# Order of the matmul engine's instructions in a hybrid decoder step: scheduled against written out

## The chip, the cores and the metric

The kernel runs on one core of a Trainium2 chip. The metric is the device time of one execution in microseconds (us). The engines are TensorE (PE, with its weight loads listed apart as PEld), VectorE (DVE), ScalarE (ACT), GpSimd (POOL) and SyncE (SP, which only issues DMAs here). Each engine works through its own instructions in the order in which the built program has them, and waits at an instruction until the semaphores that it needs have their value.

## The reference

One step of a decoder layer, for a prompt of 512 tokens and, separately, 8 decode sequences of 4 tokens. Both share the weights, so the kernel runs the projections on 544 columns. All data is float32.

```python
u = jnp.einsum('btd,dc->btc', x, w_in)            # 2048 x 18952: 13 parts side by side
h_m, C, n, m = _mlstm(q_m, k_m, v_m, ig, lf, C0, n0, m0)   # 4 heads of 512, matrix memory C
h_a = _swa_prompt(q_a, k_a, v_a, slopes, sinks)   # 32 heads of 64, window 128, 4 KV heads
hn = layernorm_per_head(h_m) * mlstm_norm_w
y = (sigmoid(g_m) * ((hn * sigmoid(o_m) * silu(z_m)) @ w_proj_m)
     + sigmoid(g_a) * ((h_a * silu(z_a)) @ w_proj_a))
out = layernorm(2 ** 0.25 * x + y @ w_out) * ln_w + ln_b
```

The decode sequences use the same formulas with a state C of 512 x 512 per sequence and head (32 of them, 1 MB each), which is read, updated and written, and with a window of 128 stored keys and values.

## The kernel before

**Precision.** Every operand of a large product is split into a high part in a reduced format and a low part, the remainder: ACT casts (`wh`, L188) and DVE subtracts (`wl`, L189). A product is then hi x hi, hi x lo and lo x hi, that is three matmuls.

**The long stage.** After a prologue, in which values and keys of the attention (L514 to L529) and the gates are projected, `paired()` (L627) works through 72 pairs of weight column blocks. A pair multiplies two blocks of 128 columns at once with seven products in place of eight (a Strassen scheme). So it has seven steps, numbered 0 to 6, with the moving operands `a11`, `s1`, `n2`, `xk` (first half), `n3`, `s4`, `xk` (second half). `half_product()` (L582) issues one step: 16 matmuls with `wh` (L593, "hi") and 8 with `wl` (L595, "lo"), each of 272 columns. Steps 0, 1, 3 and 5 accumulate in the two banks of a PSUM tile X (step 0 and 3 in the first, 1 and 5 in the second); steps 2, 4 and 6 in a tile Y. `gather()` (L597) takes the results out: L604 after step 0 (`p`), L612 after 1, L615 after 2, L617, L619, L621 and L623 (the last, after 6). `prepare()` (L563) makes `wh` and `wl` of a step up to three steps ahead; there are two buffers of each.

The pairs carry a list of work: 16 query pairs (their end, `end_qz` L754, makes the query tiles `q` by L763 and L764 and the gate `sz` by L768 and L769), merge gates, and values, keys, queries and output gates of the four mLSTM heads.

**Work between the steps.** `tick()` (L126) runs after each step and lets every live generator go one `yield` further. Three generators matter. `attentions()` (L774) takes the 16 query pairs in turn: `attention()` (L682) handles two heads, a = 0 and 1. For each head it computes scores of four query blocks j, two of them in one PSUM tile of the pool `psB` (four buffers): two matmuls per block (L700), and DVE's read with bias, minimum and sink (L702). Exponentials (L711) and division (L717) on ACT, transposes (L728) and the product with the values (L738) follow some ticks later. `samples()` (L1093) runs `sample_head()` (L1040) for the decode states: per state four matmuls with the state (L1073), four outer products (L1079) and their additions to the state (L1080), with a DMA of the next state and stores of the last. `gates_` computes the gates once.

**What sets the order.** A scheduler with a timing model orders the instructions of every engine by priority and by when it expects operands. `high_priority(offset=...)` raises the priority of a block, `issue_after(...)` adds an edge that puts instructions behind a given one on the same engine. In `tick()` such an edge keeps the small work behind the last matmul of the step just issued (`state["end"]`); later than that it may slip freely, and the steps themselves may be interleaved. DMAs are issued from SP in order.

**After the long stage** come the attention's output projection with the prompt's mLSTM in its ticks, the merge, the last projection and the layernorm. The change does not touch their code.

Of the kernel before, what the change touches and what calls it, by code (L numbers as in the profile page):

```python
# [22 lines left out]
NB = 8  # L23
# [50 lines left out]
def _build(tc, nc, i, o, es):  # L74
# [11 lines left out]
    V, A, G, PE = nc.vector, nc.scalar, nc.gpsimd, nc.tensor  # L86
# [12 lines left out]
    def nm(s):  # L99
        count[0] += 1  # L100
        return f"{s}_{count[0]}"

    def sm():
        return psB.tile([128, 512], F32, tag="sm", name=nm("sm"))
# [10 lines left out]
    def blk(ap, n=4):  # L115
        return ap.rearrange("p (b x) -> p b x", b=n)


    live = []

    def spawn(g):
        live.append(g)

    state = {}

    def tick():  # L126

        with ExitStack() as place:
            if state.get("end"):
                place.enter_context(tc.issue_after(state["end"].ins))  # L130
            for g in list(live):
                if next(g, StopIteration) is StopIteration:
                    live.remove(g)

    def drain():
        while live:
            tick()
# [137 lines left out]
    for g in range(4):  # L275
# [9 lines left out]
        for q in range(4):  # L285
# [4 lines left out]
            k = g * 4 + q  # L290
# [156 lines left out]

    def attn_values(kk, vt):

        pt, pt2 = sm(), sm()  # L450
        for b in range(4):
            PE.transpose(pt[:, b * 128:b * 128 + 128], vt[:, b * 128:b * 128 + 128], ident)
        PE.transpose(pt2[:32, 0:128], vt[:, SEQ:T], ident)
        cs = slice(kk * 128, kk * 128 + 128)
        vr, vs = ev(512), ev(128)
        A.copy(vr[:], pt[:])
        V.tensor_copy(vs[:32], pt2[:32, 0:128])
        nc.sync.dma_start(d_vr[0:SEQ, cs].rearrange("(b p) c -> p b c", p=128), blk(vr[:]))
        nc.sync.dma_start(d_vr[SEQ:T, cs], vs[:32])
        nc.sync.dma_start(vb_p[0].rearrange("t k d -> t (k d)")[:, cs], vr[:, 384:512])  # L460

    def attn_keys(kk, kt):
        nc.sync.dma_start(d_ka[kk], kt[:])
        pt = sm()
        PE.transpose(pt[:, 0:128], kt[:, 384:512], ident)
        PE.transpose(pt[:32, 128:256], kt[:, SEQ:T], ident)
        cs = slice(kk * 128, kk * 128 + 128)
        kr = ev(256)
        V.tensor_copy(kr[:, 0:128], pt[:, 0:128])
        V.tensor_copy(kr[:32, 128:256], pt[:32, 128:256])  # L470
        nc.sync.dma_start(kb_p[0].rearrange("t k d -> t (k d)")[:, cs], kr[:, 0:128])
        nc.sync.dma_start(d_ks[:, cs], kr[:32, 128:256])
# [41 lines left out]
    for kk in range(2):  # L514
        ps = gemm(win, VA_ + kk * 128, xh, xl, raws=((raw0[0], raw0[1]), (raw0[2], None))[kk], every=4, prio=150 * kk,
                  before=gates_between if kk else None)
        if kk == 0:
            spawn(x_sums())
            gates_ps = mm()
        vt = ev()  # L520
        with ahead_of_sums():
            A.copy(two(vt[:]), pv(ps))
            attn_values(kk, vt)
    for kk in range(2):
        ps = gemm(win, KA + kk * 128, xh, xl, every=4, prio=150)
        kt = ev()
        with ahead_of_sums():
            A.copy(two(kt[:]), pv(ps))
            attn_keys(kk, kt)  # L529
    drain()  # L530
    for src, dst in ((d_ks, kb_s), (d_vr[SEQ:T], vb_s)):
        nc.sync.dma_start(dst[:, 124:128].rearrange("b t k d -> b t (k d)"), src.rearrange("(b t) c -> b t c", t=NTS))
# [49 lines left out]
    def half_product(w, n):  # L582
        bank = BANK[n]
        if n == 0:
            w["X"] = mm()
        if n == 2:
            w["Y"] = mm()
        ps = w["Y"][:, 0, :HT] if bank == 2 else w["X"][:, bank, :HT]
        wh, wl = w.pop(("hl", n))
        x, first = XS[n], n in (0, 1, 2)  # L590
        for k in range(8):
            for p in range(2):
                PE.matmul(ps, wh[:, k], x(p, k), start=(first and k == 0 and p == 0), stop=False, skip_group_check=True)  # L593
        for k in range(8):
            state["end"] = PE.matmul(ps, wl[:, k], x(0, k), start=False, stop=(k == 7), skip_group_check=True)  # L595

    def gather(w, n):  # L597

# [175 lines left out]
    def attentions():  # L774
        while gates_ in live:
            yield
        for _ in last:
            pass
        esG.close()
        sp["pz"] = pool(esQ, "pz", 1)  # L780
        open_attention()
        state["open"] = True
        for k in range(16):
            if k % 4 == 0:
                kv = kv_head(k // 4)
            while k not in waiting:
                yield
            yield
            yield
            yield from attention(k, *waiting.pop(k), kv)  # L790
            state["done"] = k + 1
        esB.close()
        yield from sample_attention()
        esT.close()
        open_samples()
        state["samples"] = True
# [224 lines left out]
    def sample_finish(h, r, pC):  # L1021
        qc = w512()
        A.activation(qc[:], pC[:], AF.Copy, scale=colT2[:, 4, 1, h:h + 1])
        gs = st1([128, 4, NS], "gs", p="sw")
        nc.sync.dma_start(gs[:], d_g[h * 4:h * 4 + 4, :, SEQ:T].rearrange("c p t -> p c t"))
        yield
        num, den = r["num"], r["den"]
        pI = sm()
        PE.matmul(pI[:NS, :], cc[:, C_SEL:C_SEL + 32], qc[:], start=True, stop=True)
        V.tensor_tensor(out=num, in0=pI[:NS, :], in1=num, op=ALU.add)  # L1030
        hn = w512()[:32]
        layernorm_rows(NS, den[:, 9:10], colT2[0:32, 4, 0, h:h + 1], [num], hn, sp["sw"])
        yield
        pt = sm()
        for c in range(4):
            PE.transpose(pt[:, c * 32:c * 32 + 32], hn[:, c * 128:c * 128 + 128], ident[:32, :32])
        V.tensor_tensor(out=gs[:], in0=blk(pt[:, 0:128]), in1=gs[:], op=ALU.mult)
        nc.sync.dma_start(d_brm[h * 4:h * 4 + 4, :, SEQ:T].rearrange("c p t -> p c t"), gs[:])

    def sample_head(h):  # L1040
        r = {}
        nxt = load_C(h, 0)
        yield from sample_prep(h, r)
        pC, stores = None, []

        def store():

            with tc.issue_after(state["load"].ins):
                for dst, src in stores:
                    nc.sync.dma_start(dst, src)  # L1050
            stores.clear()

        for b in range(NB):
            ct = nxt

            qz = st1([128, 4, NS], "qz", p="sw")
            G.memset(qz[:], 0.0)
            G.tensor_copy(qz[:, :, b * 4:b * 4 + 4], r["qs"][:, :, b * 4:b * 4 + 4])
            Ab = st1([128, 512], "Ab", F32R)
            G.tensor_scalar(Ab[:], r32(r["kA"][:]), cc[:, C_M8 + b:C_M8 + b + 1], None, op0=ALU.mult)  # L1060
            for j in range(4 + b % 2):
                yield
                if j == 0:
                    store()
                elif j == 2 and b + 1 < NB:
                    with tc.issue_after(state["load"].ins):
                        nxt = load_C(h, b + 1)
            if b == 0:
                pC = sm()

            with tc.high_priority(offset=3000):
                for c in range(4):
                    PE.matmul(pC[c * 32:c * 32 + 32, :], qz[:, c], ct[:, c],  # L1073
                              start=(b == 0), stop=(b == NB - 1), tile_position=(0, c * 32))
            for c in range(4):
                if c == 2:
                    yield
                pu = sm()
                PE.matmul(pu[:], Ab[:, c * 128:c * 128 + 128], r["V4"][:], start=True, stop=True)  # L1079
                V.scalar_tensor_tensor(ct[:, c], ct[:, c], dcb[:, h, b:b + 1], pu[:], op0=ALU.mult, op1=ALU.add)  # L1080
                if c % 2:
                    stores.append((C_s[b, h, (c - 1) * 128:c * 128 + 128, :].rearrange("(c p) v -> p c v", p=128),
                                   ct[:, c - 1:c + 1]))
        yield
        store()
        while h not in gated:
            yield
        yield from sample_finish(h, r, pC)
# [75 lines left out]
    work = [fill.pop(0) for _ in range(3)]  # L1164
# [11 lines left out]
    last = last_sum(s4)  # L1176
# [1 line left out]
    spawn(gates_)  # L1178
    spawn(attentions())
    spawn(samples())  # L1180
    paired(work, last)
    state["end"] = None
    drain()

    def branch(src, p, tmp, ahead=()):

# [186 lines left out]
    for ct in range(16):  # L1373
        sg = c5t()
        nc.sync.dma_start(sg[:], d_sga[ct])
        ps = gemm(wa_, ct * 128, bah, bal, every=2)
# [12 lines left out]
    for ct in range(16):  # L1389
# [3 lines left out]
        ps = gemm(wm, ct * 128, bmh, bml)  # L1393
# [136 lines left out]
    for ct in range(16 - G3):  # L1530
# [5 lines left out]
        ps = gemm(wo, ct * 128, yh, yl, cols=CUT, raws=raws)  # L1536
# [6 lines left out]
    for g in range(G3):  # L1543
        ct = 16 - G3 + g
        ps = sm()
        for half in range(2):
            raw = load_half(wo, ct * 128, half)
            if g < 2:
                wh, wl = (w[:, :, g] for w in w2[half])
                hilo(raw[:], wh, wl)  # L1550
            else:
                w1.append(split(raw))
                wh, wl = w1[half]
# [39 lines left out]
```

## Time and profile before

| quantity | us |
|---|---|
| median of three runs | 2601.6 |
| lowest and highest run | 2598.32, 2604.69 |
| profiled execution, own time | 2600.3 |
| its span, first to last instruction | 2598.5 |

The profile is of one execution. Its page lists busy time per engine. Views of the trace give the same for chosen stretches (windows), the waits between engines (who waited for which line's result: us in total, times, longest), and the instructions in order of time (timeline). A matmul's end in the trace is modelled: matmuls of one stream overlap in the listing, and the distance of their starts is what a matmul costs. Busy time of PE therefore holds some 0.15 us beyond the point at which a next matmul could have started.

In the long stage a step of 24 matmuls follows the next, with small groups of matmuls of the generators between or, where the scheduler chose so, inside them.

### The profile page before, as it was taken

To read this page: it belongs to the slowest core of one execution; us is meant where nothing else is said; L and a number is where in the kernel's file an instruction comes from. 1 tells how busy PE (TensorE), PEld (TensorE's weight loads), DVE (VectorE), ACT (ScalarE), POOL (GpSimd) and SP (SyncE) were. 2 spreads that over 40 slices of the span, in tenths; PEclk is the share of its full clock that TensorE was granted. 3 is DMA by queue.
4 is the path that set the end of the run, shared out by engine and by line. 5 is a ranking of instruction groups with operands and counts; after the bars stand their busy time and mean duration, and the time that the engine had idled before them with its cause. 6 is when DMAs were issued, how large, how long until landed. Compare 5 with 4: busy or idle time off the path is not lost.

```text
span 2598.5 us, 48858 instructions
## 1 busy us (share of the span) xinstructions
PE 2539.5 (98%) x19994; PEld 2469.6 (95%) x19994; DVE 1711.2 (66%) x2508; ACT 1176.7 (45%) x1908; POOL 359.9 (14%) x334
## 2 busy tenths in 40 slices
PE   8999999999999999999999999999999999999997
PEld 8999999999999999999999998999999999999997
DVE  7867667676676777587777777777766553333335
ACT  4447666666666665343433443434633332222221
POOL 2111111111111111121112222211000000000002
PEclk9999999999999999999999999999999999999999
DMA  6566656666665655457577566576755455445432
GB/s 194 136 150 160 151 138 155 150 145 144 151 151 138 149 133 146 107 179 229 163 219 235 151 207 212 157 229 200 222 181 172 156 170 163 132 140 178 116 93 90
DMA packets 537103, 421.86 MB, mean 162 GB/s; under 512 B 43536, under 2 KB 449344, under 8 KB 536592
## 3 DMA queue, kind: packets, MB, share of 16 engines
q1 hardware_dynamic: 526800, 382.04, 49.8%
q0 software_dynamic: 10080, 36.70, 8.2%
q8 instruction: 157, 2.57, 0.4%
q14 instruction: 66, 0.54, 0.1%
HBM read 297.66 MB, written 86.42 MB: 148 GB/s over the span
## 4 chain that ended last, share of the span: by engine, by line
PE 61%; DVE 2%; ACT 1%; issue 0%; DVEq 0%; ACTq 0%
PE mm L197 21%; PE mm L593 20%; PE mm L595 9%; PE sm L1256 2%; PE sm L1079 1%; PE sm L1073 1%; PE sm L1288 1%; PE sm L1301 1%; ACT wh L188 1%; PE sm L197 1%; DVE raw L570 0%; DVE z L1495 0%; PE sm L898 0%; PE sm L897 0%; PE sm L1235 0%
## 5 line engine op out<-in xcount | busy, mean ns | idle before, releaser
L188 ACT CAST wh<-raw 128x1024 fp32r<-128x1024 f32 x604 | 632.7, 1049 | 989.2 <-PE mm L593 568.2
L189 DVE TENSOR_TENSOR wl<-raw,wh 128x1024 fp32r<-128x1024 f32 x604 | 765.2, 1272 | 443.0 <-ACT wh L188 425.3
L593 PE MATMUL mm<-xk,wh 128*128 128x272 f32 x2304 | 314.4, 288 | 3.4 <-ACT ev L612 2.4
L593 PEld LDWEIGHTS mm<-xk,wh 128*128 128x128 f32 x2304 | 298.5, 188 | 8.0 <-ACT ev L612 3.1
L570 DVE TENSOR_TENSOR raw<-raw,raw 128x1024 f32<-128x1024 f32 x218 | 267.0, 1228 | 4.8 <-DMA raw<-in_w_in 2.6
L197 PE MATMUL mm<-bh,wl 128*128 128x272 f32 x1024 | 214.1, 289 | 0.0
L197 PE MATMUL mm<-bh,wh 128*128 128x272 f32 x1024 | 213.6, 290 | 0.0
L197 PE MATMUL mm<-bl,wh 128*128 128x272 f32 x1024 | 213.3, 288 | 0.0
L613 POOL TENSOR_TENSOR ev<-p,ev 128x272 f32<-128x272 f32 x72 | 103.6, 1439 | 588.4 <-ACT ev L612 562.5
L593 PE MATMUL mm<-n2h,wh 128*128 128x272 f32 x576 | 154.6, 300 | 25.0 <-ACT wh L188 24.7
L595 PE MATMUL mm<-xk,wl 128*128 128x272 f32 x1152 | 173.9, 288 | 0.0
L197 PEld LDWEIGHTS mm<-bh,wh 128*128 128x128 f32 x1024 | 160.7, 188 | 2.3 <-issue 2.3
L197 PEld LDWEIGHTS mm<-bl,wh 128*128 128x128 f32 x1024 | 161.3, 188 | 0.0
L197 PEld LDWEIGHTS mm<-bh,wl 128*128 128x128 f32 x1024 | 160.9, 189 | 0.0
L595 PEld LDWEIGHTS mm<-xk,wl 128*128 128x128 f32 x1152 | 155.7, 188 | 0.4
L593 PE MATMUL mm<-s1h,wh 128*128 128x272 f32 x576 | 151.0, 294 | 4.0 <-ACT p L604 4.0
L593 PE MATMUL mm<-n3h,wh 128*128 128x272 f32 x576 | 150.3, 290 | 0.2 <-DVE ev L615 0.2
L593 PE MATMUL mm<-n3l,wh 128*128 128x272 f32 x576 | 150.3, 291 | 0.0
L593 PE MATMUL mm<-n2l,wh 128*128 128x272 f32 x576 | 150.1, 292 | 0.0
L593 PE MATMUL mm<-s4h,wh 128*128 128x272 f32 x576 | 149.0, 290 | 1.1 <-ACT ev L617 1.1
L593 PE MATMUL mm<-s1l,wh 128*128 128x272 f32 x576 | 149.8, 292 | 0.0
L593 PE MATMUL mm<-a11h,wh 128*128 128x272 f32 x576 | 149.3, 290 | 0.4 <-DVE t L409 0.4
(427 smaller groups left out, 5515.1 us busy)
## 6 DMA issues: line engine op xcount, KB each, us to landing
raw<-in_w_in SPq DMA_DIRECT2D x296, 512.0 KB
raw<-raw POOLq DMA_DIRECT2D x70, 512.0 KB, 4.9
C<-in_state_mlstm_C SPq DMA_DIRECT2D x32, 1024.0 KB
out<-C SPq DMA_DIRECT2D x64, 512.0 KB
raw<-in_w_proj_a SPq DMA_DIRECT2D x32, 512.0 KB
raw<-in_w_proj_m SPq DMA_DIRECT2D x32, 512.0 KB
raw<-in_w_out SPq DMA_DIRECT2D x32, 512.0 KB
d_sgm<-ev SPq DMA_DIRECT2D x16, 272.0 KB
```

The source lines that it names most:

```text
L188: A.copy(wh[:], raw[:])
L189: V.tensor_tensor(out=wl[:], in0=raw[:], in1=r32(wh[:]), op=ALU.subtract)
L197: PE.matmul(ps[:, f, :w], a[:, kk], b(k, c, w), start=(k == 0 and n == 0), stop=(k == 15 and n == 2))
L570: V.tensor_tensor(out=w[out][:], in0=w[a][:], in1=w[b][:], op=ALU.add)
L593: PE.matmul(ps, wh[:, k], x(p, k), start=(first and k == 0 and p == 0), stop=False, skip_group_check=True)
L595: state["end"] = PE.matmul(ps, wl[:, k], x(0, k), start=False, stop=(k == 7), skip_group_check=True)
L613: G.tensor_tensor(out=c22, in0=p1, in1=c11, op=ALU.subtract)
L1073: PE.matmul(pC[c * 32:c * 32 + 32, :], qz[:, c], ct[:, c], start=(b == 0), stop=(b == NB - 1), tile_position=(0, c * 32))
L1079: PE.matmul(pu[:], Ab[:, c * 128:c * 128 + 128], r["V4"][:], start=True, stop=True)
L1256: PE.matmul(pp[:, 0:258], a[:, b * 128:b * 128 + 128], b_[:, b, f], start=(b == 0 and n == 0), stop=(b == 3 and n == 2))
L1288: PE.matmul(pp[:, 0:n], x_[c][:, b * 128:b * 128 + 128], y_[c][:, b * 128:SEQ], start=(c == 0 and m == 0), stop=(c == 3 and m == 2))
L1301: PE.matmul(pp[:, 0:258], x_[:, off:off + 128], y_[:, b, f], start=(b == 0 and n == 0), stop=(b == j and n == 2))
```

## The change

The long stage, from the first pair to the drain behind the last, is put under `tc.manual_schedule(engines={PE.engine})`: PE takes its instructions in the order in which the source issues them. The other engines are scheduled as before. The edge in `tick()` and the raised priority of the state's matmuls are taken out.

The numbers of `yield`s change: the first attention of each KV head starts after four ticks and not two; `sample_finish` gets one more tick ahead of its first matmul and two more ahead of its transposes; each decode state takes four ticks ahead of its matmuls, where odd states had five.

In the prologue the values' and keys' transposes become generators of their own, which start two ticks later, and are no longer raised in priority.

```diff
     def tick():
-
-        with ExitStack() as place:
-            if state.get("end"):
-                place.enter_context(tc.issue_after(state["end"].ins))
-            for g in list(live):
-                if next(g, StopIteration) is StopIteration:
-                    live.remove(g)
+        for g in list(live):
+            if next(g, StopIteration) is StopIteration:
+                live.remove(g)
...
     def attn_values(kk, vt):
 
+        yield
+        yield
         pt, pt2 = sm(), sm()
...
     def attn_keys(kk, kt):
         nc.sync.dma_start(d_ka[kk], kt[:])
+        yield
+        yield
         pt = sm()
...
         with ahead_of_sums():
             A.copy(two(vt[:]), pv(ps))
-            attn_values(kk, vt)
+        spawn(attn_values(kk, vt))
...
         with ahead_of_sums():
             A.copy(two(kt[:]), pv(ps))
-            attn_keys(kk, kt)
+        spawn(attn_keys(kk, kt))
...
         for k in range(8):
-            state["end"] = PE.matmul(ps, wl[:, k], x(0, k), start=False, stop=(k == 7), skip_group_check=True)
+            PE.matmul(ps, wl[:, k], x(0, k), start=False, stop=(k == 7), skip_group_check=True)
...
             while k not in waiting:
                 yield
-            yield
-            yield
+            for _ in range(2 if k % 4 else 4):
+                yield
             yield from attention(k, *waiting.pop(k), kv)
...
         nc.sync.dma_start(gs[:], d_g[h * 4:h * 4 + 4, :, SEQ:T].rearrange("c p t -> p c t"))
         yield
+        yield
         num, den = r["num"], r["den"]
...
         layernorm_rows(NS, den[:, 9:10], colT2[0:32, 4, 0, h:h + 1], [num], hn, sp["sw"])
-        yield
+        for _ in range(3):
+            yield
...
-            for j in range(4 + b % 2):
+            for j in range(4):
                 yield
...
-            with tc.high_priority(offset=3000):
-                for c in range(4):
-                    PE.matmul(pC[c * 32:c * 32 + 32, :], qz[:, c], ct[:, c],
-                              start=(b == 0), stop=(b == NB - 1), tile_position=(0, c * 32))
+            for c in range(4):
+                PE.matmul(pC[c * 32:c * 32 + 32, :], qz[:, c], ct[:, c],
+                          start=(b == 0), stop=(b == NB - 1), tile_position=(0, c * 32))
...
-    paired(work, last)
-    state["end"] = None
-    drain()
+
+    with tc.manual_schedule(engines={PE.engine}):
+        paired(work, last)
+        drain()
```

## The prediction

> **What bounds the kernel now.** The page comes first: which engine has no time left.
>
> ```profile
> span 2598.5 us, 48858 instructions
> PE 2539.5 (98%) x19994; PEld 2469.6 (95%) x19994; DVE 1711.2 (66%) x2508; ACT 1176.7 (45%) x1908; POOL 359.9 (14%) x334
> ```
>
> PE is busy for 98% of the span, so the time is PE's work plus the gaps in it: 59 us of gaps in all. The busy times by stage (windows of us; PE, PEld, DVE, ACT, POOL, clock, DMA share, GB/s) show where they lie. 350 to 990 holds nearly all of the attention, 990 to 1862 the decode states.
>
> ```profile
> 350.00:990.00 640.00, 620.90 (x4967) 617.61 (x4966) 451.17 (x705) 407.83 (x747) 108.69 (x89) 0.99 0.62 148
> 990.00:1862.00 872.00, 864.48 (x6708) 809.70 (x6708) 661.56 (x800) 362.41 (x480) 167.32 (x158) 0.99 0.63 188
> ```
>
> So PE lacks 19 us in the first and 8 us in the second. That is all an edit of PE's order could win there; what it could lose has no such bound. PE's waits name the cause:
>
> ```profile
> PE mm L593 <- ACT wh L188: 24.9, 38, 2.3
> PE mm L593 <- ACT p L604: 4.0, 2, 3.6
> PE sm L452 <- ACT ev L522: 2.4, 1, 2.4
> ```
>
> 38 of them are one event, once per pair, which the timeline shows at a typical place (start us, us, engine, line):
>
> ```profile
> 527.73 0.43 DVE L623 SCALAR_TENSOR_TENSOR ev<-mm,p 128x272 f32<-128x272 f32 x1
> 528.20 1.34 ACT L763 ACTIVATE q<-ev 64x544 fp32r<-64x544 f32 x2 [1.34 <-DVE ev L623]
> 528.27 1.16 PE L595 MATMUL mm<-a11h,wl 128*128 128x272 f32 x8
> 529.56 1.04 ACT L188 CAST wh<-raw 128x1024 fp32r<-128x1024 f32 x1
> 530.63 0.40 ACT L604 ACTIVATE p<-mm 128x272 f32<-128x272 f32 x1
> 530.66 0.39 PE L593 MATMUL mm<-n2h,wh 128*128 128x272 f32 x1 [1.23 <-ACT wh L188]
> ```
>
> Eight matmuls in 1.16 with the last one lasting 0.29 are 0.125 apart, so a step of 24 takes 3.0 us. After step 0 (a11), PE could go on at 529.28. It goes to step 2 (n2), ahead of step 1 (s1), and waits for n2's cast, which stands behind two query casts. Why step 2 first? Step 1 writes the second bank of the tile X, and its first matmul waits until L604 has copied step 0's result out of that tile. The scheduler's order hides this copy behind step 2. I count 1.38 us lost here, 0.15 more than the 1.23 listed, since the listing counts from the modelled end of the last matmul; over 38 waits 24.9 + 38 x 0.15 = 31 us.
>
> **Part 1: PE in source order.** The built order of the changed kernel (instructions per engine and the semaphore that each awaits) settles what moves. No matmul is added or removed. All 72 pairs now run steps 0 to 6 in turn, hi before lo, and each tick's small work stands in one piece between two steps.
>
> *(a) Step 2's wait goes.* Its cast now has step 1 as cover, 3.0 us against at most 2.3 waited: -31 us. The other end: half stays, -15.
>
> *(b) Step 1's wait comes out of its cover.* In 45 of 72 pairs nothing stands between the lo part of step 0 and step 1; in the other 27 transposes or sample work does. The trace has a bare one:
>
> ```profile
> 141.31 0.79 PE L595 MATMUL mm<-a11h,wl 128*128 128x272 f32 x5
> 142.14 0.40 ACT L604 ACTIVATE p<-mm 128x272 f32<-128x272 f32 x1 [0.88 <-PE mm L595]
> 142.59 0.19 PEld L593 LDWEIGHTS mm<-s1h,wh 128*128 128x128 f32 x1 [0.70 <-ACT p L604]
> ```
>
> The next matmul was due at 141.31 + 5 x 0.125 = 141.94 and came at 142.59: 0.65 lost with ACT free at once. In 16 of the 45, the pairs after a query pair, ACT has the queue of the 528 us rows: queries, cast, then L604, ending at 531.03, so step 1 would start at 531.08, 1.8 after it was due, and the first matmul after a wait takes 0.1 more (0.39 against 0.29). Sum 16 x 1.9 + 29 x 0.65 = 49 us; ends 45 x 0.65 = 29 and, with ACT late everywhere, 45 x 1.9 = 86. Behind the wait stands all of PE, and nobody else gains by it.
>
> In the 27 covered pairs nothing is lost: seven transposes there last 0.93 (504.83 to 505.76 by the next row), about L604's latency.
>
> ```profile
> 504.83 0.93 PE L728 MATMUL sm<-cc,s 128*128 128x128 f32 x7
> 505.03 0.40 ACT L604 ACTIVATE p<-mm 128x272 f32<-128x272 f32 x1 [2.92 <-DVE raw L570]
> ```
>
> By the Trainium skill (PSUM — Partial Sum Buffer, "PSUM bank collisions raise a hardware error") accesses to different banks do not collide, so step 1 need not wait for a read of the other bank, and the sum would be 49 us less, about 2650. The row at 142.59 disagrees with this kernel's semaphores: PE did wait for L604.
>
> *(c) The scores.* attention() writes two query blocks j into one PSUM tile, and DVE reads each (L702) before PE may write the next into the same tile. The old order put the eight L700 of a head into pairs and fours with other matmuls between. Now they stand as 2, wait, 4, wait, 2. There are 16 attentions of two heads: 32 stretches, 64 waits. The rows for one:
>
> ```profile
> 536.04 1.23 DVE L189 TENSOR_TENSOR wl<-raw,wh 128x1024 fp32r<-128x1024 f32 x1 [3.99 <-ACT wh L188]
> 537.18 0.34 DVE L702 CUSTOM_DVE_ANT_0 s<-sm,nb,nsinkb 128x128 f32<-128x128 f32 x1
> 537.45 0.08 DVE L702 DVE_READ_ACCUMULATOR2_ANT mn<- 128x1 f32 x1
> 540.30 0.40 PE L700 MATMUL sm<-k,q 128*128 128x256 f32 x2
> 540.38 0.48 DVE L702 CUSTOM_DVE_ANT_0 s<-sm,nb,nsinkb 128x256 f32<-128x256 f32 x1 [0.28 <-PE sm L700]
> 540.79 0.08 DVE L702 DVE_READ_ACCUMULATOR2_ANT mn<- 128x1 f32 x1
> 540.79 0.48 DVE L702 CUSTOM_DVE_ANT_0 s<-sm,nb,nsinkb 128x256 f32<-128x256 f32 x1
> 541.20 0.08 DVE L702 DVE_READ_ACCUMULATOR2_ANT mn<- 128x1 f32 x1
> ```
>
> Two matmuls take 0.40; DVE starts 0.03 after the end of such a pair (the pair of 539.95, ended 540.35); a narrow read lasts 0.35 (537.18 to 537.53), two wide ones 0.90 (540.38 to 541.28); from a release to PE's matmul I take 0.06 (530.60 to 530.66). With DVE free: 0.40 + 0.03 + 0.35 + 0.06 = 0.84 until block 1; 0.43 until DVE reads it, 0.90 for blocks 1 and 2, 0.06: block 3 at 2.23, and PE is out at 2.47. Without waits eight take 0.96. Lost 1.5, and 0.1 for each slow first matmul: 1.7. In 29 of 32, the built DVE order has one low part (L189, 1.23) between the reads of block 0 and block 1: DVE is then free at 0.78 + 1.23 = 2.01 in place of 1.27, so 2.45. In the last three the low part stands ahead of block 0: 1.7 + 1.23 = 2.9. Sum 29 x 2.45 + 3 x 2.9 = 80 us; ends 32 x 1.7 = 54 and 32 x (1.7 + 2 x 1.23) = 133.
>
> *(d) The clock.* Windows of 3.41 us, the clock being the third column from the end:
>
> ```profile
> 380.09:383.50 3.41, 1.22 (x10) 1.00 (x9) 3.32 (x4) 2.74 (x4) 0.00 (x0) 1.00 0.52 105
> 383.50:386.92 3.42, 3.42 (x18) 3.42 (x16) 0.43 (x1) 1.04 (x1) 0.00 (x0) 0.50 0.27 81
> 431.29:434.70 3.41, 2.18 (x18) 1.96 (x17) 2.92 (x4) 1.94 (x3) 0.00 (x0) 1.00 0.62 148
> 434.70:438.12 3.42, 3.42 (x30) 3.42 (x29) 0.00 (x0) 1.94 (x2) 0.00 (x0) 1.00 0.03 10
> ```
>
> A window with PE busy for 1.22 us is followed by one at half clock, with 18 matmuls in place of 30: 12 x 0.125 = 1.5 us. Busy 2.18 is not. The long step-2 waits cause three such in the trace (0.99 in the stage row); they go with (a): -4.5. A score stretch has some 1.9 us of idle by modelled ends, so a window that holds it all is busy for 1.5, between the two rows. I take 4 of 32, +6; ends 0 and 32 x 1.5 = 48. The Trainium skill (TensorE: Matmul & The Clock Gate, "Part 1: The HAM clock gate") lets the clock drop after at least one idle window; by it no stretch would drop it and the sum would be 6 less. The row with 1.22 us of work disagrees.
>
> **Part 2: later steps.** The values' transposes wait 2.4 us for L522's copy; two ticks later the copy is done: -2.4, other end 0. Their stores (d_vr, vb_p, kb_p, d_ks; d_ka stays) move two ticks back in SP's queue behind weight loads; the first score row starts at 193.1 us by the view of L702, long after, so nothing. The attentions' extra steps, sample_finish's and one tick less per odd state shift the sample work earlier. DVE carries it with 661.56 of 872 us, and PE's only listed wait at L1073 is small:
>
> ```profile
> L702 DVE CUSTOM_DVE_ANT_0 s<-sm,nb,nsinkb x128: 339/480/485, 193.1 to 939.1; 128x256 f32<-128x256 f32 x96, 128x128 f32<-128x128 f32 x32
>   issue: 2.4, 16
> ```
>
> C's load and its stores keep their tick numbers from the previous state's end; POOL's qz and Ab have four ticks, 12 us, where POOL is busy 19%. If that cover went, the 0.15 per wait of this row (2.4 / 16) would come once per state: 32 x 0.15 = 5. I take 0, ends -2.4 and +5.
>
> **Sum** against the profiled run's own 2600.3 (span 2598.5 and 1.8 around it): 2600.3 + 49 + 80 - 31 - 4.5 + 6 - 2.4 = 2697. The median of the runs is 1.3 above the profiled one: 2699.
>
> **Rivals.** *Faster:* the 31 us go and the 109 new waits (45 + 64) find their results ready. It decides at (31 + 4.5 + 2.4) / 109 = 0.35 us per wait; below it the kernel wins, down to 2562. Against it: the bare row lost 0.65 and a score wait spans a DVE read of 0.35 at least. 0.03. *Step 1 does not wait* for L604, which reads bank 0 while step 1 writes bank 1: 2699 - 49 = 2650; against it the 142.59 row; 0.04. *DVE late at the scores:* two low parts in each stretch, 32 x 1.23 = 39 more, 2738; for it DVE's 70% (451 of 640), against it that low parts are ready early when PE stalls. 0.13. *The clock falls after each stretch:* 42 more, 2741; for it the 380.09 row, against it the 431.29 row; 0.13. *The order does not change in effect* (PE catches up from its queue): 2600, 0.02, against it the built order.
>
> **Numbers.** The forecast's own case, 2645 to 2725 (the low ends of (b) and (c): 2600.3 + 29 + 54 - 31 - 4.5 - 2.4 = 2645), has 0.62, the five rivals 0.35, and 0.03 is left for what I have not thought of. With the clock's and DVE's rivals the range is 2640 to 2770. Faster by over 0.2% (about what a measurement of this kernel can tell from no change) 0.03, the same 0.02, slower 0.95.
>
> **What would show it.** Right: PE's waits list the scores (sm L700 <- L702) with 64 times and 60 to 80 us, L593 <- L604 with some 45 times and 25 to 45 us (listed idle is 0.15 short), and wh L188 nearly gone; the loss lies between 350 and 990 us (+75), the later stage grows by 10 to 15. Wrong: score waits under 0.4 us each, L604 waits in fewer than 20 pairs, or a new wait for wl L189 or for C in the sample stage that is larger than these. More half-clock windows than about ten would move the clock from a side term to a main one.

## The result and the profile after

| | median us | runs | lowest and highest | ratio to before, 95% interval |
|---|---|---|---|---|
| before | 2600.0 | 4 | 2598.32, 2604.69 | |
| changed | 2724.7 | 4 | 2720.51, 2725.66 | 1.0473 [1.0455, 1.0492] |

The change makes the kernel 4.7% slower: 2724.7 where 2699 was predicted. That lies inside the range, at the upper end (2725) of the forecast's own case. The page of the changed kernel has the same matmuls in a span that is 123.5 us longer:

```profile
span 2722.0 us, 48851 instructions
PE 2575.7 (95%) x19994; PEld 2493.5 (92%) x19994; DVE 1713.2 (63%) x2508; ACT 1188.6 (44%) x1908; POOL 363.7 (13%) x334
```

PE's share falls from 98% to 95%, and its busy time itself grows by 36 us with no matmul added. The first is waiting, the second is mostly slower matmuls. PE's waits (us in total, times, longest) give the first:

```profile
PE sm L700 <- DVE mn L702: 62.9, 64, 2.8
PE mm L593 <- ACT p L604: 47.4, 47, 4.1
PE sm L1038 <- ACT w L925: 4.8, 2, 3.9
PE sm L964 <- POOL rep L959: 3.8, 1, 3.8
...
PE mm L193 <- ACT ev L522: 2.4, 1, 2.4
```

The 38 waits for `wh` are gone from the list, and two long lines have come. Where in time the loss lies is read from two lines: the first L834 (the decode part of the attention, behind all scores) and the last L593. Before:

```profile
L834 PE MATMUL sm<-cc,kb x16: 272/273/329, 983.9 to 997.2; 128*128 128x128 f32 x16
...
L593 PE MATMUL mm<-xk,wh x2304: 282/287/397, 96.4 to 1860.8; 128*128 128x272 f32 x192
```

After (first and last start stand ahead of the shapes):

```profile
L834 PE MATMUL sm<-cc,kb x16: 272/273/329, 1082.8 to 1096.1; 128*128 128x128 f32 x16
...
L593 PE MATMUL mm<-xk,wh x2304: 282/287/595, 96.8 to 1984.6; 128*128 128x272 f32 x192
```

1082.8 - 983.9 = 99 us are lost with the scores, 1984.6 - 1860.8 - 99 = 25 in the decode states, nothing behind. One place of the timeline shows both new waits (start us, us, engine, line):

```profile
569.78 0.79 PE L595 MATMUL mm<-a11h,wl 128*128 128x272 f32 x5
...
571.77 0.40 ACT L604 ACTIVATE p<-mm 128x272 f32<-128x272 f32 x1
...
572.22 0.40 PE L593 MATMUL mm<-s1h,wh 128*128 128x272 f32 x1 [1.65 <-ACT p L604]
...
575.35 0.34 PE L700 MATMUL sm<-k,q 128*128 128x128 f32 x2
...
575.73 0.35 DVE L702 CUSTOM_DVE_ANT_0 s<-sm,nb,nsinkb 128x128 f32<-128x128 f32 x1 [2.53 <-PE sm L700]
...
576.00 1.22 DVE L185 TENSOR_TENSOR wl<-raw,wh 128x1024 fp32r<-128x1024 f32 x1
...
576.14 0.74 PE L700 MATMUL sm<-k,q 128*128 128x256 f32 x4 [0.45 <-DVE mn L702]
577.14 0.48 DVE L702 CUSTOM_DVE_ANT_0 s<-sm,nb,nsinkb 128x256 f32<-128x256 f32 x1
...
577.54 0.48 DVE L702 CUSTOM_DVE_ANT_0 s<-sm,nb,nsinkb 128x256 f32<-128x256 f32 x1
...
578.08 0.50 PE L700 MATMUL sm<-k,q 128*128 128x256 f32 x2 [1.20 <-DVE mn L702]
...
578.43 0.29 PE L593 MATMUL mm<-n2h,wh 128*128 128x272 f32 x1
```

Step 1 was due at 569.78 + 5 x 0.125 = 570.41 and came at 572.22: 1.81 lost, behind the copy L604, which ACT reached late. Then the stretch of scores: 2, wait, 4, wait, 2. From its first matmul to step 2's it takes 578.43 - 575.35 = 3.08; without waits 0.96. DVE had a low part of weights (L185) between its reads.

The second loss is in the windows of 3.41 us (the clock is the third column from the end):

```profile
526.07:529.48 3.41, 1.57 (x11) 1.23 (x11) 2.65 (x8) 3.11 (x10) 0.00 (x0) 1.00 0.49 115
529.48:532.90 3.42, 3.42 (x17) 3.42 (x16) 0.83 (x4) 2.83 (x10) 0.00 (x0) 0.50 0.80 216
580.68:584.10 3.42, 1.82 (x14) 1.48 (x12) 1.79 (x4) 2.70 (x7) 0.00 (x0) 1.00 0.46 90
584.10:587.51 3.41, 2.41 (x10) 2.41 (x11) 1.63 (x9) 2.14 (x8) 0.00 (x0) 0.50 1.00 279
587.51:590.92 3.41, 3.41 (x17) 3.41 (x17) 0.15 (x1) 1.41 (x4) 0.00 (x0) 0.50 0.00 0
```

Here a window in which PE works for 1.57 or 1.82 us is followed by one at half clock, and where waits fall into that too, by a second. (Not every window with so little work is: see the last section.) The trace before has 7 halved windows in the long stage, the trace after 23, in 17 stretches of one or two. Of the 23, 12 stand behind waits of the scores, 4 behind waits for L604 (one of them, at 116.5 us, as before), 3 behind the waits of L964 and L1038, and 4 in the decode attention behind windows that list no idle time (3 before). The three behind step 2's cast are gone.

To divide the loss I took, for every two successive matmuls of PE, the distance of their starts less the usual distance of these two lines in the profile before, and added these excesses up by what the second matmul waited for (long stage, us):

| excess | before | changed |
|---|---|---|
| step 2 for its cast | 31.3 | 0 |
| step 1 for L604 | 4.4 | 56.5 |
| scores | 0 | 72.1 |
| matmuls in halved windows | 10.3 | 33.6 |
| sample_finish's L1038, sample_prep's L964 | 0 | 8.9 |
| other gaps between two steps | 5.5 | 1.4 |

The differences sum to 121 of the stage's 124 us. How the pairs of lines are grouped moves a row by up to some 2 us.

### The profile page after: what moved, and what is told of

Read it like the earlier page. It is cut to its first block, busy times and chain, and to the rows that moved or that the text cites. A ratio compares the mean times of both kernels' runs of the same rounds, so it can differ in the third digit from the quotient of the medians.

```text
span 2722.0 us, 48851 instructions
## 1 busy us (share of the span) xinstructions
PE 2575.7 (95%) x19994; PEld 2493.5 (92%) x19994; DVE 1713.2 (63%) x2508; ACT 1188.6 (44%) x1908; POOL 363.7 (13%) x334
## 4 chain that ended last, share of the span: by engine, by line
PE 51%; DVE 3%; ACT 1%; issue 1%; DMA 0%; POOL 0%; DVEq 0%; SPq 0%; ACTq 0%
PE mm L193 20%; PE mm L593 16%; PE mm L595 7%; PE sm L1258 2%; PE sm L1080 1%; PE sm L1290 1%; PE sm L1074 1%; PE sm L1303 1%; PE sm L193 1%; DVE wl L185 1%; DVE raw L570 0%; ACT wh L184 0%; DVE z L1497 0%; PE sm L1237 0%; PE sm L1313 0%
## 5 line engine op out<-in xcount | busy, mean ns | idle before, releaser
L185 DVE TENSOR_TENSOR wl<-raw,wh 128x1024 fp32r<-128x1024 f32 x604 | 749.6, 1242 | 426.4 <-ACT wh L184 406.2
L593 PE MATMUL mm<-xk,wh 128*128 128x272 f32 x2304 | 322.4, 294 | 0.0
L593 PEld LDWEIGHTS mm<-xk,wh 128*128 128x128 f32 x2304 | 307.4, 194 | 2.7 <-ACT wh L184 0.8
L570 DVE TENSOR_TENSOR raw<-raw,raw 128x1024 f32<-128x1024 f32 x218 | 276.8, 1271 | 4.7 <-DMA raw<-in_w_in 1.1
L193 PE MATMUL mm<-bh,wl 128*128 128x272 f32 x1024 | 214.0, 289 | 0.0
L193 PE MATMUL mm<-bh,wh 128*128 128x272 f32 x1024 | 213.6, 290 | 0.0
L193 PE MATMUL mm<-bl,wh 128*128 128x272 f32 x1024 | 213.3, 288 | 0.0
L593 PE MATMUL mm<-s1h,wh 128*128 128x272 f32 x576 | 159.3, 307 | 47.5 <-ACT p L604 47.4
L593 PEld LDWEIGHTS mm<-s1h,wh 128*128 128x128 f32 x576 | 112.0, 194 | 61.1 <-ACT p L604 60.8
L193 PEld LDWEIGHTS mm<-bh,wh 128*128 128x128 f32 x1024 | 160.7, 188 | 2.3 <-issue 2.3
L193 PEld LDWEIGHTS mm<-bl,wh 128*128 128x128 f32 x1024 | 161.4, 188 | 0.0
L193 PEld LDWEIGHTS mm<-bh,wl 128*128 128x128 f32 x1024 | 160.9, 189 | 0.0
L593 PE MATMUL mm<-s1l,wh 128*128 128x272 f32 x576 | 152.6, 296 | 0.0
L593 PE MATMUL mm<-n2h,wh 128*128 128x272 f32 x576 | 152.1, 295 | 0.0
L593 PE MATMUL mm<-n2l,wh 128*128 128x272 f32 x576 | 151.6, 295 | 0.0
L593 PE MATMUL mm<-n3h,wh 128*128 128x272 f32 x576 | 150.9, 293 | 0.0
L593 PE MATMUL mm<-n3l,wh 128*128 128x272 f32 x576 | 150.6, 293 | 0.0
L593 PE MATMUL mm<-s4h,wh 128*128 128x272 f32 x576 | 149.0, 290 | 0.3 <-ACT ev L617 0.3
```

What stands on the lines that cost most here:

```text
L185: V.tensor_tensor(out=wl[:], in0=raw[:], in1=r32(wh[:]), op=ALU.subtract)
L193: PE.matmul(ps[:, f, :w], a[:, kk], b(k, c, w), start=(k == 0 and n == 0), stop=(k == 15 and n == 2))
L570: V.tensor_tensor(out=w[out][:], in0=w[a][:], in1=w[b][:], op=ALU.add)
```

## The experiments

Times are medians; the kernel before, beside them on the same chip, had 2600.5 to 2602.4. "Excess" is that of the table above.

### The two waits alone and together

`e1_reads_behind_both`, on the changed kernel: both blocks of a score tile are multiplied, then read.

```diff
                     PE.matmul(pp[:, c0 + w0:c0 + 256], ...)
-                V.tensor_tensor_reduce(s_[:, j, w0:256], ...)
+                if j % 2 == 0:
+                    continue
+                for jj in (j - 1, j):
+                    w0, c0 = (128 if jj == 0 else 0), (jj % 2) * 256
+                    V.tensor_tensor_reduce(s_[:, jj, w0:256], ...)
```

> The changed kernel, with the two blocks of a score tile multiplied first (four L700) and DVE's two reads issued behind them, so that no matmul waits for a read of its own tile. Theory (the 63 score waits cost 72 us by the starts of PE's matmuls, and the half-clock windows of the attention stage some 15 us on top of those that the kernel before has): 2724.7 - 72 - 15 = 2638, range 2625 to 2655, no L700 <- L702 left and fewer than 10 half-clock windows in the attention stage. Rival 1 (DVE is late with its reads, so the wait moves on to the next user of a score tile): a new PE wait for L702 of 20 us or more, and a time over 2680. Rival 2 (clock is independent of these waits): 2653 with the half-clock windows all still there.

`e2_copy_behind_step1`, on the changed kernel: L604 is issued behind step 1, and step 3, the next to write that bank, has step 2 as cover.

```diff
             with tc.high_priority(offset=AHEAD):
-                gather(w, n)
+                if n == 1:
+                    gather(w, 0)
+                if n > 0:
+                    gather(w, n)
```

> The changed kernel, with the copy L604 of step 0's result issued behind step 1's matmuls, so that step 1 does not wait for it; step 3, which writes that bank next, has the whole of step 2 as cover. Theory (55 waits of step 1 cost 56 us by starts): 2724.7 - 55 = 2670, range 2655 to 2682, no wait of step 1 for L604. Rival 1 (the copies are late by ACT's queue, so step 3 takes the wait over): L593 <- L604 or L612 keeps 30 us or more, time over 2700. Rival 2 (the rigid order costs by itself and the listed wait only covers it): time over 2715 though the wait is gone.

`e3_both` has both edits.

> Both edits on the changed kernel. Theory (the two waits and the clock that falls with them are the whole loss, and the gain of the changed order, 31 us of waits for step 2's cast, comes out when they are gone): 2724.7 - 72 - 55 - 20 = 2578, range 2562 to 2600, under the kernel before. Rival (part of the loss lies in the rigid order itself or in the moved steps): over 2615.

| kernel | median us | ratio, 95% interval |
|---|---|---|
| e1 | 2641.3 | 1.0150 [1.0130, 1.0170] |
| e2 | 2673.1 | 1.0277 [1.0262, 1.0293] |
| e3 | 2568.0 | 0.9876 [0.9859, 0.9892] |

The longest of PE's waits in e1, and then in e2 (whose lines are numbered 3 higher from the edit on, so that L703 is L700):

```profile
PE mm L593 <- ACT p L604: 51.1, 47, 4.1
PE sm L1042 <- ACT w L929: 4.7, 2, 3.9
```

```profile
PE sm L703 <- DVE mn L705: 62.6, 64, 2.8
PE sm L1041 <- ACT w L928: 5.4, 2, 3.9
...
PE mm L593 <- ACT ev L612: 0.8, 1, 0.8
```

Each edit takes its own wait away and leaves the other; neither wait moves on to a next place (the new lines are 1.1 us and less). All three times are in the range of their theory. e1 gains 83 us, 72 of waits and the rest clock (excess in the attention stage 22.8 to 6.6, less what the waits for L604 and the decode stage grow). e2 gains 52, less than the 56.5 of its waits, since its clock gets worse: 27 halved windows in place of 23. Together they gain 157, more than the 135 of the single ones, since with both gone hardly any window is halved (5 in the long stage; 16 in e1). The written order without these two waits is 32 us faster than the kernel before. That is close to the 31 us of step 2's waits, which the change did win, but small items stand on both sides: the 4.4 us for L604 and part of the clock's 10.3 go too, and the 9 us of L1038 and L964 come on top.

### The clock by itself

`e11_waits_filled`, on the changed kernel: four matmuls into a tile that nobody reads stand inside each score wait. They add 32 us of work where PE idled.

```diff
+                if j == 1:
+                    spare = sm()
+                if j % 2:
+                    for kx in (k1, k2, k1, k2):
+                        PE.matmul(spare[:, 0:256], qs[a][:, j * 128:j * 128 + 128], kx[:, k0:k0 + 256], start=True, stop=True)
```

> The changed kernel (2724.7; 17 stretches at half clock in the long stage, 23 us lost to them in the attention stage) with four more matmuls, whose result nobody reads, in each of the 64 score waits: 0.5 us of work inside a wait of 1 us, so that PE is less idle and the waits end at the same time. Theory (the clock falls when PE is idle for more than about half of a 3.41 us window, so the halved windows of the attention stage go): listed score waits down by 64 x 0.5 = 32 to some 31 us, half-clock stretches from 17 to 9 or fewer, time 2724.7 - 16 = 2709, range 2700 to 2716, although 256 matmuls are added. Rival (the halved windows have another cause): 2721 or more with as many of them, or slower by part of the 32 us of work added.

Measured: 2698.8 us, 1.0383 [1.0368, 1.0399]. 256 matmuls more make the kernel 26 us faster. Its PE waits:

```profile
PE mm L593 <- ACT p L604: 47.4, 47, 4.1
PE sm L705 <- DVE mn L707: 24.1, 36, 0.7
```

L705 is L700 here. L604's line is the same to a tenth. Halved stretches fall from 17 to 7, and the clock's excess from 33.6 to 14.2, that is 19 of the 26 us; the rest is the score excess, which with the filling counted (32.8 + 32) is 7 below 72.1. The theory is right, its size a little small (2698.8 lies 1 us under its range). The filling does to the windows what it was meant to do: in the attention stage the changed kernel has 15 windows at full clock with less than 1.85 us of work, e11 has 3.

`e6_waits_apart`, on e2's kernel, tries to get there by spreading: a step between block 1 and block 2 of a head, for which the free steps behind scores and softmax go.

```diff
                 V.tensor_tensor_reduce(s_[:, j, w0:256], ...)
+                if j == 1:
+                    yield
             st.append((s_, mx, mn, sums, h))
             yield
-        yield
...
             yield
-        yield
         for a in range(2):
             s_ = st[a][0]
```

> The kernel of e2_copy_behind_step1 (2673 us, 22 half-clock windows, 28 us lost to them in the attention stage by the starts of PE's matmuls), with one step of 24 matmuls between block 1 and block 2 of a head, so that the two score waits of a stretch fall into different windows; the free steps behind the scores and behind the softmax are taken out, so that the number of steps is the same. Theory (a window is halved when one ahead of it holds too much idle time, and a whole stretch of two waits is what it takes): still 64 score waits and 55 to 73 us, half-clock windows down to fewer than 9, time 2673 - 22 = 2651, range 2640 to 2662. Rival (a single wait is enough, or the windows come from something else): 15 or more half-clock windows, 2665 or more.

Measured: 2678.6 us, 1.0294 [1.0278, 1.0309]; 19 halved stretches. The theory fails and the rival is right. The waits and two pairs of windows:

```profile
PE sm L703 <- DVE mn L705: 78.2, 64, 4.0
```

```profile
361.74:365.15 3.41, 1.51 (x13) 1.30 (x12) 2.39 (x5) 1.38 (x2) 0.00 (x0) 1.00 0.50 144
365.15:368.57 3.42, 3.42 (x18) 3.42 (x17) 1.46 (x5) 1.32 (x6) 0.86 (x1) 0.50 0.31 59
...
351.50:354.91 3.41, 1.59 (x13) 1.39 (x12) 1.95 (x4) 1.37 (x3) 0.38 (x1) 1.00 0.80 154
354.91:358.33 3.42, 3.34 (x26) 3.34 (x27) 0.86 (x6) 2.45 (x7) 0.00 (x0) 1.00 0.46 113
```

Each wait now stands right behind a step's end, where DVE has the step's gather and a low part to do first; one wait alone empties a window down to 1.51 us of work, and that is enough. The window with 1.59 us kept the clock, and so did one with 1.54 (from 1006.86 us).

### The order and the moved steps

`e4_steps_only` is the kernel before with part 2 alone, `e5_order_only` with part 1 alone; `e12_early_start` is the changed kernel whose attentions start as before:

```diff
-            for _ in range(2 if k % 4 else 4):
+            for _ in range(2):
                 yield
```

> The kernel before with only the changed numbers of steps between dependent parts (values' and keys' transposes two steps later included); the scheduler orders PE as before. Theory (these edits carry none of the loss): 2600 with 6 to either side, 2594 to 2606. Rival (the sample stage's growth of 25 us comes from the moved steps): 2612 or more, with the growth behind the attention.

> The kernel before with PE in source order alone (no steps moved, prologue as before). Theory (the order carries the loss; the moved steps can only soften waits of the sample stage under it): score waits and step-1 waits as in the changed kernel, 64 and about 47 of them, and 2725 plus longer waits for the four layernorms of sample_finish, which have one step of 3 us in place of three (up to 6 us each, 24 together): 2720 to 2750. Rival (the moved steps themselves lengthen the order written out): below 2715.

> The changed kernel (2724.7), in which the first attention of each KV head starts after two steps, as in the kernel before, and not four; all else as changed. It is to tell why the order alone (2757) loses 32 us more than with the moved steps, of which 11 are waits for the layernorm and 19 more half clock in the attention stage. Theory (the position of the score waits against the 3.41 us windows of the clock decides how many windows are halved, and the start after four steps moves it): half-clock loss in the attention stage from 23 to some 42 us, 2724.7 + 19 = 2744, range 2735 to 2752; score waits and layernorm waits unchanged. Rival (the start of the attention does not matter): 2719 to 2730.

| kernel | median us | ratio, 95% interval |
|---|---|---|
| e4 | 2609.5 | 1.0035 [1.0022, 1.0048] |
| e5 | 2757.2 | 1.0593 [1.0577, 1.0608] |
| e12 | 2733.7 | 1.0512 [1.0495, 1.0530] |

e4 lies between its two expectations, and e12 too (2735 and 2730); e5 lies 7 us above the range of its theory, which had no term for more loss by the clock. The PE waits of e4 (lines 4 higher):

```profile
PE mm L597 <- ACT wh L188: 29.6, 42, 5.0
PE mm L597 <- ACT p L608: 5.1, 3, 4.1
```

The 9 us are not in the decode states, as the rival had it: the excess grows by 6 for step 2's cast, about 1 for the copy and 2.5 in gaps behind transposes, and the first matmul behind the attention (L834 of before) comes 10 us later. Under the scheduler the moved steps are a small loss; under the order written out they are a gain of 2757 - 2725 = 32 us. Of this, 11 stand in PE's waits of e5 (lines 4 lower: L696 is L700, L1032 the transposes of sample_finish):

```profile
PE sm L696 <- DVE mn L698: 66.1, 64, 3.1
PE mm L589 <- ACT p L600: 49.3, 44, 4.0
PE sm L1032 <- ACT w L921: 15.6, 4, 4.8
```

The layernorm of sample_finish is late four times for 15.6 us, where the longer steps leave 4.8. Another 19 us are clock: excess 53.0 against 33.6, all of it in the attention, with the same number of score waits. e12, which lacks only the start after four steps, loses 8 of these 19 again (attention 22.8 to 30.9, where 42 was expected). So where the waits lie against the clock's windows matters; the other 11 us were not traced to an edit.

### Why the scheduler ran step 2 first

`e9_before_with_copy` is the kernel before with e2's edit, `e10_before_with_reads` with e1's, `e8_before_with_both` with both.

> The kernel before, ordered by the scheduler, with the two edits of e3_both (reads behind both blocks, copy of step 0 behind step 1). Theory (the scheduler puts step 2 ahead of step 1 because step 1 waits for the copy; without that wait it keeps the source's order, and the 31 us of waits for step 2's cast go): 2600 - 31 - 4 = 2565, range 2558 to 2582. Rival (its order has other reasons): 2592 or more, with 30 or more waits for wh.

> The kernel before, ordered by the scheduler, with only the copy L604 of step 0 behind step 1's matmuls. Theory (this copy alone made the scheduler put step 2 ahead of step 1, and the scores cost it nothing): the waits for wh go, 2600 - 47 = 2553, range 2547 to 2562, as with both edits. Rival (the score reads also cost the scheduler's order something): 2566 or more.

> The kernel before, ordered by the scheduler, with only DVE's score reads behind both blocks. Theory (the scheduler already covers the score reads with other matmuls): 2600 with 6 to either side, some 38 waits for wh as before. Rival (their cover costs the scheduler something elsewhere): 2590 or less.

| kernel | median us | ratio, 95% interval | pairs with step 2 ahead of step 1 |
|---|---|---|---|
| before | 2600.5 | | 58 of 72 |
| e10 | 2598.1 | 0.9994 [0.9984, 1.0004] | 58 |
| e8 | 2553.0 | 0.9810 [0.9794, 0.9826] | 0 |
| e9 | 2550.7 | 0.9808 [0.9794, 0.9823] | 0 |

The longest waits of PE in the long stage of e9:

```profile
PE mm L593 <- ACT wh L188: 1.8, 1, 1.8
...
PE mm L593 <- DVE ev L621: 0.8, 1, 0.8
...
PE mm L593 <- ACT ev L617: 0.3, 1, 0.3
```

One copy issued a step later wins 50 us. The scheduler had avoided L604 at the price of step 2's cast; without that wait it keeps the source's order of the steps, and still covers the score reads by itself (e10: no difference). The 50 are more than the 31 of the cast, since the 4.4 for L604 go too and the long stage has one halved window left of 7; e8, for which 35 were reckoned, lies 5 us below the range of its theory. e9 beats both kernels of this study and e3. Against the best written order (e7, below) it is 5 us ahead, and there the intervals overlap.

### What is left of the written order

`e7_both_later_finish` is e3 with the two rows of the decode states mended:

```diff
-        for _ in range(3):
+        for _ in range(5):
             yield
         pt = sm()
...
         G.tensor_copy(rep[:], ks_[:].unsqueeze(2).to_broadcast([128, 4, 4, NS]))
         yield
+        yield
```

> The kernel of e3_both (2568) with two more steps ahead of sample_finish's transposes and one more ahead of sample_prep's first matmul. Theory (the three waits for the layernorm and for the repeated keys, 9.5 us by starts, and the two half-clock windows behind them, 4 to 6 us, are mere lateness): 2568 - 9.5 - 5 = 2554, range 2548 to 2561. Rival (they hide other work that is then waited for, or the sample work runs past the last pair): 2565 or more.

Measured: 2555.9 us, 0.9815 [0.9799, 0.9832]: 12 us less than e3, as theory had it within 2. The waits for the layernorm go and those for the repeated keys fall to 0.8 us. So the rows of 4.8 and 3.8 us in the changed kernel were mere lateness. Of e3's 4 halved windows behind these waits 1 is left; but the profiled run of e7 has 4 in place of 1 behind windows without idle time in the decode attention, so it doesn't show a gain in the clock. With three edits the written order comes within 5 us of what e9 has with one.

## Why the prediction came out as it did

The side, the two waits and their mechanism were right; the clock was a side term in it and turned out a main one. Step by step:

- **(a) Step 2's wait goes, -31.** Measured -31.3 by starts. Right: the line is gone from PE's waits.
- **(b) Step 1's wait, +49.** Measured 56.5 - 4.4 = +52. (e2 gained 52 as well, but by chance: 56.5 of waits less some 5 of clock.) Right, with the pairs divided otherwise: the 45 bare pairs are there, 25 of them at 0.65 to 0.9, but 8 at 1.1 to 1.5, 8 at 1.6 to 1.8 (16 at 1.9 were assumed) and 4 at 2.8 to 4.3. Listed were 47 times and 47.4 us, against "some 45" and 25 to 45.
- **(c) The scores, +80.** Measured 72.1 in 64 waits, 2.25 per stretch where 2.45 was taken; the stretch at 575.35 lost 3.08 - 0.96 = 2.12. Right, a tenth too large: in that stretch DVE is at block 1 at 577.14, 1.79 behind the first matmul, where 2.01 was reckoned.
- **(d) The clock, +1.5 net.** Measured 33.6 - 10.3 = +23. This is the term that was mis-sized. It took 4 halved windows for 32 stretches, from one row on each side (1.22 us of work dropped the clock, 2.18 did not). The trace after has rows of 1.57 and 1.82 that drop it, so many more stretches qualify: 12 windows are halved behind scores where 4 were taken. The new L604 waits of 2.8 us, which (d) left out, halve three more (those that begin at 631.9, 853.7 and 1966.5 us), and the waits of L964 and L1038 another three. "More half-clock windows than about ten would move the clock from a side term to a main one" is what happened: 23. That the slower matmuls, and not a wait that comes with them, cost this is shown by e11.
- **Part 2, -2.4.** The transposes' wait of 2.4 was not won: the row L193 <- ACT ev L522 has the same 2.4 us, so the matmul behind now waits for the same copy. The zero taken for the sample work missed the 8.9 us of L1038 and L964.
- **The sum was closer than its parts.** By e5 the order alone costs 2757 - 2602 = 155 where the sum without part 2 had 100, and the moved steps give back 32 where 2.4 was reckoned. Both errors are mainly clock and layernorm waits, and they partly cancel: that the sum came within 26 us is in part luck. Of these 26, the clock is 22, L1038 and L964 9, part 2 and (b) 5; the scores and other gaps take back some 12, and 2 are not placed.
- **The bound on a gain.** The prediction reads the 19 and 8 us that PE lacks as all that an edit of its order could win. e9 shows that this is no bound: from 86 us to the first L834 (983.9 us) PE of the kernel before lacked 27 us, and e9 is there 34 us earlier. Busy time also counts the modelled end of a matmul ahead of each wait, and matmuls at half clock.
- **Place.** Predicted +75 with the attention and +10 to 15 later; measured 99 and 25. The clock is in both, the two L964 and L1038 waits in the second.

The rivals: "step 1 does not wait" is ruled out by the row at 572.22 and by e2: PE waits for the read of the first bank before it writes the second. That wait is one that the program asks for; no run shows what the banks would do without it. "DVE late" would have made the score term larger than 80; it is smaller. "The clock falls after each stretch" is half right: its price was 42, and the clock's excess over the kernel before is 23. "Faster" fails on 1.0 us per listed wait against its 0.35, and "the order does not change in effect" on the two new rows of waits.

## What to carry to other kernels

Before an order is pinned, look in the source for a read of a tile that stands just ahead of the next write into it (another block, another bank): here the scheduler had been hiding these, and the written order made bare waits of all 64 at the scores and of 45 of 72 at step 1. Moving the copy one step later cost nothing here, where another tile is written in between, and it helped the scheduled kernel as well, because that had paid for the detour elsewhere. Waits of PE should be priced with the clock: here 23 of 124 us came from matmuls that ran slower after the wait was over.

## What the runs showed of the hardware that was not expected

- **Useless matmuls can pay.** 256 of them, in waits, took 26 us off (e11).
- **The clock falls on a part of a window.** Windows with 1.51 (e6), 1.57 and 1.82 us of work out of 3.41 were followed by half clock; others with 1.54 and 1.59 (e6) were not. In the changed kernel itself four windows with 1.76 or 1.77 us kept it, each with one wait of about 1.65 us for L604. One holds the 1.81 us lost at 570.41:

```profile
570.44:573.85 3.41, 1.76 (x15) 1.64 (x14) 2.67 (x3) 1.68 (x3) 0.00 (x0) 1.00 0.57 154
573.85:577.27 3.42, 2.58 (x20) 2.22 (x18) 1.54 (x4) 2.70 (x4) 1.23 (x1) 1.00 0.00 0
```

The windows with 1.75 to 1.82 us that were followed by half clock hold two waits of the scores. So the border is not sharp in these modelled busy times, but lies far above an idle window; what decides between two such windows stays open.
- **A full window can be followed by half clock too.** These two of the changed kernel follow each other:

```profile
1154.12:1157.53 3.41, 3.41 (x31) 2.94 (x31) 2.03 (x3) 0.44 (x2) 1.13 (x3) 1.00 0.08 17
1157.53:1160.95 3.42, 3.42 (x17) 3.42 (x17) 0.35 (x2) 0.37 (x2) 0.00 (x0) 0.50 0.47 137
```

The first lists PE busy throughout. Of its 31 matmuls 23 are small ones of the decode attention, with 32 moving columns in place of 272 and tiles of 128x64 or 32x64 in place of 128x128 (0.23 us each as modelled); that these count for less is a guess, and no run tried it.
